# Moving the tiles of a one-core decoder step to other addresses in on-chip memory

## The chip, the cores and the metric

The kernel runs on one core of one Trainium2 chip. A core has engines that run side by side, each through its own list of instructions: TensorE (matrix products, PE in the profile, with its weight loads as PEld), VectorE (DVE), ScalarE (ACT), GpSimd (POOL) and SyncE (SP, which here issues most of the transfers). They share an on-chip memory of 128 partitions, called SBUF. A tile has one address, in bytes, which is the same in each partition. The metric is the device time of one execution, in microseconds (us).

## The reference

The reference is one inference step of a decoder layer, for 1024 prompt tokens and 8 x 8 sample tokens that share the weights, with a model width of 1024, all in 32-bit floats:

```python
u = rmsnorm(x); a, q, k, v, g_a, g_b = split(u @ w_in)
A = (multiscale_mean(a) - a) -> linear per group -> scale -> @ w_pa     # windows 2, 4, 8, 16
B = combine(dilated_attention(q_g, k_g, v_g) for g in 3 groups) @ w_pb  # (128,1) (512,4) (2048,16)
h = x + (sigmoid(g_a) * A + sigmoid(g_b) * B) @ w_o
y = h + relu(rmsnorm(h) @ w_up)**2 @ w_down
```

It also returns updated pooling rows and key and value windows for the prompt and for each sample.

## The kernel before, in words

Tokens are columns. The 1088 tokens stand in the free dimension, 1024 + 64, and a quarter of them is 272 columns. Nearly all the time goes into matrix products in TensorE's faster 32-bit format (`float32r` in the program). To keep the accuracy, each operand is split into a high and a low part, and each product is made of three passes, high x high, high x low and low x high (`PASSES`). A pass of one 128 x 128 block of weights over 272 tokens is one matmul instruction, which comes with one weight load. The operand that is loaded into the array is called stationary here, and the one that is streamed through it moving.

The stages, in order: the pooling projection (`pool_input`, line 326, tile `a`); queries, keys and values for the three attention groups with the attention around them (`gemm`, line 198, tiles `pq`, `pk`, `pv`, `pqk`); the two gates (`products`, line 1286, tile `pg`); the two branch projections (line 1592, `pab`); the output projection (`gemm`, `ph`); the up projection (`products`, `pz`); the down projection (line 2050, `pd`). Gates, up and down projection use a seven-product scheme in place of eight for a 2 x 2 division of the matrices. It forms sums of weight blocks and of activation blocks; the summed activations are called T1 to T4 in the code.

The tiles that the change touches, and where they stand:

- `places` (line 109) is the resident tile for weights, 48 KB of each partition, on the left side of the memory. Its three parts are filled in turn by ScalarE (high part) and VectorE (low part). Later the same bytes are reused at other offsets (`spots`) for weight blocks, for the sums T2 and T3, and in the down projection for the activations.
- `act_t` (line 83) are two tiles on the right side, high and low part of the activations. They are moving operand in `a`, `pg`, `ph`, `pz` and part of `pab`, and stationary operand in the query, key and value products of two of the groups.
- `ab0` (right side, below `act_t`) is moving operand in half of `pab`. `natt` (right side too) holds a copy of the activations that is the stationary operand for the first attention group.
- `xms`, `rtok`, `xeps` (lines 70 to 72) are seven small tiles of 9 columns with statistics per token, on the left side ahead of `places`.

A pool on the left side is stacked upwards and one on the right side downwards, in the order in which they are opened. A tile takes a multiple of 32 bytes. So the size of an early tile sets the address of all tiles opened after it on its side. Before the change, `places` stands at byte 21184, which is 192 over a multiple of 256, and 0 over a multiple of 64. The two activation tiles stand at 159712 and 194528, which is 224 over a multiple of 256 and 32 over a multiple of 64. A block of 128 in the contraction is 4352 bytes away from the next one in an activation tile, which is 17 x 256, and a quarter of the tokens is 1088 bytes, 17 x 64. So every address of a moving operand in the activation tiles is 32 over a multiple of 64 before the change. In `places` every operand starts at a multiple of 64.

The order of TensorE's work is the order of the code (the scheduler is told to leave that engine alone). The other engines' order is made by a scheduler.

Of the kernel before, what the change touches and what calls it, by code (L numbers as in the profile page):

```python
# [7 lines left out]
F32 = mybir.dt.float32  # L8
# [7 lines left out]
P = 128  # L16
# [20 lines left out]
def decoder_step(ctx, tc, i, o):  # L37
# [5 lines left out]
    def pool(name, bufs=1, **kw):  # L43
        return ctx.enter_context(tc.tile_pool(name=name, bufs=bufs, **kw))
# [9 lines left out]
    cp = pool("const")  # L54
# [12 lines left out]
    mhalf = cp.tile([P, 8], F32, name="mhalf")  # L67
    wqs = cp.tile([P, 6], F32, name="wqs")
    wqk = cp.tile([P, 6], F32, name="wqk")
    xms = cp.tile([P, 9], F32, name="xms")  # L70
    rtok = [cp.tile([P, 9], F32, name=f"rtok{g}") for g in range(3)]
    xeps = [cp.tile([P, 9], F32, name=f"xeps{g}") for g in range(3)]
    v_.memset(ones, 1.0)

    s_.activation(mhalf, ones[:, :8], AF.Copy)
# [5 lines left out]
    acts = ExitStack()  # L81
    actp = acts.enter_context(tc.tile_pool(name="act", bufs=1, side="right"))
    act_t = [actp.tile([P, KD, TOK], F32R, name=f"act{hl}") for hl in range(2)]
    act = [[t[:, k, :] for k in range(KD)] for t in act_t]
    act4 = [[t[:, k, :].rearrange("p (r l) -> p r l", r=4) for k in range(KD)] for t in act_t]

# [2105 lines left out]
```

## Time and profile before

| | |
|---|---|
| median of three runs | 1419.31 us (1417.27 to 1419.51) |
| span of the profiled execution | 1417.3 us; what lies around it can't be told from the runs, whose lowest is 1417.27 |
| TensorE busy | 1403.6 us, 99% of the span, 11101 matmuls |
| granted TensorE clock, mean | 0.998 |
| VectorE, ScalarE, GpSimd busy | 68%, 53%, 17% |
| share of the chain that ended last | PE 95%, DMA 2%, POOL 1%, ACT 1% |
| longest wait of TensorE for another engine | 3.2 us |

How to read it: the chain of waits is followed back from the last instruction, and gives each microsecond to the work that the end waited for. With 95% of it on TensorE, the time is the number of its matmuls times the spacing of their starts. The mean duration in a row (287 ns for 272 columns) is no cost, because matmuls are pipelined: the cost is the time from one start to the next. In the timeline each row gives a start, and the start of the next row less that of this one, divided by the count, is the spacing.

### The profile page before, as it was taken

The page shows a single profiled execution, that of the slowest core. Times are in us where ns is not written, and L with a number is a line of the kernel's source. Part 1 is how long each engine was busy: PE and PEld are TensorE (multiplying, and loading weights), DVE is VectorE, ACT ScalarE, POOL GpSimd, SP SyncE. Part 2 cuts the span into 40 slices and gives each one's busy share as a digit, 9 for nine tenths or more (in the row PEclk, how much of TensorE's full clock was granted, in tenths as well). Part 3 has the DMA queues.
Part 4 walks back from the last instruction along what each step waited for, and adds up shares of the span by engine and source line. Part 5 has one row for each costly group of instructions (what it writes and reads, how often), then busy time and mean ns, then how long its engine had stood idle before and what let it go on. Part 6 is the DMA issues. An engine that isn't in the chain of part 4 may idle for free.

```text
span 1417.3 us, 29517 instructions
## 1 busy us (share of the span) xinstructions
PE 1403.6 (99%) x11101; PEld 1355.2 (96%) x11101; DVE 967.3 (68%) x1766; ACT 758.0 (53%) x1962; POOL 235.6 (17%) x330
## 2 busy tenths in 40 slices
PE   9999999999999999999999999999999999999998
PEld 8988887887999999999999999999999999999998
DVE  7788666676676667876468677665665686664565
ACT  8557755777864323563336555454554545444443
POOL 0822275566500100000000000000000000000100
PEclk9999999999999999999999999999999999999999
DMA  6322789856477777965468668856758987777684
GB/s 213 116 92 104 206 219 223 206 129 143 109 251 225 247 231 236 323 226 174 132 199 288 224 219 270 263 199 209 246 191 273 326 270 259 227 244 226 204 257 167
DMA packets 184541, 303.58 MB, mean 214 GB/s; under 512 B 26567, under 2 KB 90509, under 8 KB 182350
## 3 DMA queue, kind: packets, MB, share of 16 engines
q1 hardware_dynamic: 181326, 258.04, 58.7%
q0 software_dynamic: 3072, 43.65, 9.6%
q8 instruction: 87, 1.43, 0.4%
q14 instruction: 56, 0.46, 0.1%
HBM read 231.55 MB, written 113.73 MB: 244 GB/s over the span
## 4 chain that ended last, share of the span: by engine, by line
PE 95%; DMA 2%; POOL 1%; ACT 1%; DVE 0%; issue 0%; SPq 0%; DVEq 0%; POOLq 0%; ACTq 0%
PE pz L1286 23%; PE pd L2050 23%; PE pg L1286 12%; PE ph L198 7%; PE pqk L198 6%; PE pab L1592 5%; PE pv L198 4%; PE a L326 4%; PE pq L198 2%; PE pk L198 1%; POOL pcv L849 1%; PE sg0b L682 1%; PE pog0b L715 1%; PE pl L505 1%; PE tpg0b L701 0%; POOL mr L644 0%
## 5 line engine op out<-in xcount | busy, mean ns | idle before, releaser
L2050 PE MATMUL pd<-places 128*128 128x272 f32 x2688 | 335.0, 287 | 0.5 <-DVE t L1914 0.5
L2050 PEld LDWEIGHTS pd<-places 128*128 128x128 f32 x2688 | 334.6, 188 | 0.7 <-DVE t L1914 0.7
L1293 ACT ACTIVATE places<-raw_d 128x544 fp32r<-128x544 f32 (+1 forms) x176 | 111.1, 646 | 164.3 <-DMA raw_d<-z_d 58.1
L1294 DVE TENSOR_TENSOR places<-raw_d,places 128x544 fp32r<-128x544 f32 (+1 forms) x176 | 122.9, 711 | 92.9 <-ACT places L1293 91.6
L2090 POOL DMA_DIRECT2D out_kv_sample_dram<-in_cache_kv_dram x96 | 47.2, 492 | 801.7 <-ACT places L1293 588.4
L1286 PE MATMUL pz<-act,places 128*128 128x272 f32 x1080 | 141.5, 289 | 0.0
L1286 PEld LDWEIGHTS pz<-act,places 128*128 128x128 f32 x1080 | 138.2, 188 | 0.0
L198 PE MATMUL ph<-act,places 128*128 128x272 f32 x768 | 97.0, 288 | 0.0
L198 PEld LDWEIGHTS ph<-act,places 128*128 128x128 f32 x768 | 96.5, 188 | 0.1
L1286 PE MATMUL pg<-act,places 128*128 128x272 f32 x576 | 76.6, 290 | 0.0
L1286 PEld LDWEIGHTS pg<-act,places 128*128 128x128 f32 x576 | 73.6, 188 | 0.6 <-issue 0.3
L1286 PE MATMUL pz<-places,apart 128*128 128x272 f32 x528 | 68.2, 287 | 0.0
L1286 PEld LDWEIGHTS pz<-places,apart 128*128 128x128 f32 x528 | 66.8, 188 | 0.0
L198 PE MATMUL pqk<-places,act 128*128 128x512 f32 x240 | 60.7, 403 | 0.0
L1286 PE MATMUL pz<-act,apart 128*128 128x272 f32 x456 | 59.9, 289 | 0.0
L1286 PEld LDWEIGHTS pz<-act,apart 128*128 128x128 f32 x456 | 58.3, 188 | 0.1
L198 PEld LDWEIGHTS pqk<-places,act 128*128 128x128 f32 x240 | 44.7, 192 | 9.8
L198 PE MATMUL pv<-places,act 128*128 128x256 f32 x384 | 50.4, 287 | 3.2 <-DVE places L115 3.2
L644 POOL TENSOR_TENSOR mr<-ms,mhalf 128x4 f32<-128x4 f32 (+2 forms) x39 | 53.0, 1359 | 3.1
L849 POOL TENSOR_TENSOR pck<-pck,qs 128x256 f32<-128x256 f32 x64 | 47.8, 779 | 31.6 <-DMA pck<-in_cache_kv_dram 17.1
L326 PE MATMUL a<-act,places 128*128 128x384 f32 (+1 forms) x288 | 50.8, 337 | 1.8 <-ACT places L114 1.0
L326 PEld LDWEIGHTS a<-act,places 128*128 128x128 f32 x288 | 49.2, 193 | 2.5 <-ACT places L114 1.3
(431 smaller groups left out, 2837.6 us busy)
## 6 DMA issues: line engine op xcount, KB each, us to landing
out_kv_sample_dram<-in_cache_kv_dram POOLq DMA_DIRECT2D x72, 480.0 KB, 5.0
raw_d<-z_d SPq DMA_DIRECT2D x112, 272.0 KB
z_d<-t SPq DMA_DIRECT2D x80, 272.0 KB
raw_d<-in_w_down_dram SPq DMA_DIRECT2D x80, 256.0 KB
raw_u<-in_w_up_dram SPq DMA_DIRECT2D x64, 256.0 KB
raw_qkv<-in_w_in_dram SPq DMA_DIRECT2D x36, 256.0 KB
pck<-in_cache_kv_dram SPq DMA_DIRECT2D x32, 256.0 KB
pcv<-in_cache_kv_dram SPq DMA_DIRECT2D x32, 256.0 KB
```

The source lines that it names most:

```text
L198: last_mm[0] = t_.matmul(out, lhs(a, k), rhs(b, k), start=(j == 0), stop=(j == len(terms) - 1))
L326: last_mm[0] = t_.matmul(pts[m][:, :n], wt[:, a, kk, m * P:(m + 1) * P], act4[b][kk][:, :, part4(c)], start=(p == 0 and kk == 0), stop=(p ...
L505: t_.matmul(pl[:, :npr], lin[:, g, :], dp_[:, c0:c0 + npr], start=True, stop=True)
L644: last_norm[0] = g_.tensor_tensor(r[:n, :H], ms[:n, :H], mhalf[:n, :H], op=ALU.pow)
L682: t_.matmul(sc[e][:, hp, j * P:(j + 1) * P], qT[rows, hp, :], kT[rows, 2 + hp, :], start=True, stop=True)
L849: ins = g_.tensor_tensor(out, *others, op=ALU.mult)
L1286: last_mm[0] = t_.matmul(x[c][:, :Q], A[:, a, k * P:(k + 1) * P], Bv(b, k, c), start=(first and n == 0), stop=(n == len(terms) - 1), skip_ ...
L1293: ins = s_.activation(view(t[:, 0]), src, AF.Copy)
L1294: v_.tensor_tensor(view(t[:, 1]), src, view(t[:, 0]).bitcast(F32), op=ALU.subtract)
L1592: last_mm[0] = t_.matmul(q[x][:, c, :Q], w.rearrange("p s n -> p (s n)")[:, at:at + P], rhs, start=(n == 0), stop=(n == len(terms) - 1))
L2050: last_mm[0] = t_.matmul(chain[t][:, c, :Q], A[:, a, t * P:(t + 1) * P], Z[:, b, c * Q:(c + 1) * Q], start=(fresh and f == 0 and n == 0), ...
L2090: ins = g_.dma_start(d, a)
```

## The change

Two edits, both to sizes. The seven small statistics tiles become seven slices of one tile of 64 columns: 256 bytes in place of 7 x 64 = 448 bytes. A tile of 56 columns (224 bytes) that nothing uses is opened below the activations on the right side.

```diff
-    xms = cp.tile([P, 9], F32, name="xms")
-    rtok = [cp.tile([P, 9], F32, name=f"rtok{g}") for g in range(3)]
-    xeps = [cp.tile([P, 9], F32, name=f"xeps{g}") for g in range(3)]
+    stats = cp.tile([P, 64], F32, name="stats")
+    xms, *per_token = (stats[:, 9 * n:9 * n + 9] for n in range(7))
+    rtok, xeps = per_token[:3], per_token[3:]
...
     act_t = [actp.tile([P, KD, TOK], F32R, name=f"act{hl}") for hl in range(2)]
+    actp.tile([P, 56], F32, name="act_end")
```

So every tile that is opened on the left side after `stats` moves down by 192 bytes, and every tile on the right side moves down by 224 bytes, for as long as the activations are held. `places` is then at 20992 and the activations at 159488 and 194304, all multiples of 256. `ab0` moves from 32 over a multiple of 64 to a multiple of 64, `natt` the other way, from a multiple of 64 to 32 over one. Each engine's list has the same instructions in the same order, with as many waits, before and after; only addresses differ. The names of lines below line 83 shift by one.

## The prediction

> **What bounds the kernel now.** I read the page first: busy time, granted clock and the chain that ended last.
>
> ```profile
> PE 1403.6 (99%) x11101; PEld 1355.2 (96%) x11101; DVE 967.3 (68%) x1766; ACT 758.0 (53%) x1962; POOL 235.6 (17%) x330
> PEclk9999999999999999999999999999999999999999
> PE 95%; DMA 2%; POOL 1%; ACT 1%; DVE 0%; issue 0%; SPq 0%; DVEq 0%; POOLq 0%; ACTq 0%
> ```
>
> TensorE is the bound in every stage, at full granted clock. The chain leaves 5% to other things. The list of TensorE's waits for other engines confirms it; these are its longest wait and the only one in the down projection:
>
> ```profile
> PE pv L198 <- DVE places L115: 3.2, 1, 3.2
> PE pd L2050 <- DVE t L1914: 0.5, 1, 0.5
> ```
>
> So no faster engine or transfer can give more than a few microseconds, and a change of addresses acts through one thing: the spacing of matmul starts. Two stretches of 100 us from the table by stage show how near it is to constant (columns: length, then busy time and count of PE, PEld, DVE, ACT, POOL, then clock, DMA share, GB/s):
>
> ```profile
> 500.00:600.00 100.00, 100.00 (x799) 100.00 (x799) 74.85 (x116) 40.93 (x66) 6.83 (x14) 1.00 0.80 263
> 1100.00:1200.00 100.00, 100.00 (x806) 100.00 (x805) 72.42 (x111) 47.94 (x79) 2.44 (x5) 1.00 0.86 283
> ```
>
> Nearly all of these matmuls stream 272 columns. In gates and branch projections (500 to 600 us) one takes 100/799 = 125.2 ns, in the down projection 100/806 = 124.1 ns. In the down projection both operands lie in `places`, at multiples of 64 bytes. In the gates more than half of the moving operands come from the activation tiles, which are 32 bytes off. That is the first sign of a price, about 1 ns, and the rest of the working is about what it is the price of.
>
> **The change part by part.** It removes no instruction, adds none and moves none; the lists of all engines read the same. What can change is what one instruction takes. I take the operands in groups.
>
> First, moving operands that come onto a multiple of 64. Their number is in the groups by shape:
>
> ```profile
> L1286 PE MATMUL pz<-act,places 128*128 128x272 f32 x1080 | 141.5, 289 | 0.0
> L198 PE MATMUL ph<-act,places 128*128 128x272 f32 x768 | 97.0, 288 | 0.0
> L1286 PE MATMUL pg<-act,places 128*128 128x272 f32 x576 | 76.6, 290 | 0.0
> L1286 PE MATMUL pz<-act,apart 128*128 128x272 f32 x456 | 59.9, 289 | 0.0
> L1592 PE MATMUL pab<-ab,places 128*128 128x272 f32 x384 | 50.5, 287 | 0.0
> L1592 PE MATMUL pab<-act,places 128*128 128x272 f32 x192 | 26.9, 289 | 0.0
> L1286 PE MATMUL pg<-act,gapart 128*128 128x272 f32 x192 | 25.5, 289 | 0.0
> L326 PE MATMUL a<-act,places 128*128 128x384 f32 x192 | 36.4, 351 | 1.8 <-ACT places L114 1.0 <-ACT act L304 0.9
> L326 PE MATMUL a<-act,places 128*128 128x320 f32 x96 | 14.8, 311 | 0.0
> L2050 PE MATMUL pd<-places 128*128 128x272 f32 x2688 | 335.0, 287 | 0.5 <-DVE t L1914 0.5
> ```
>
> With 272 columns that is 1080 + 768 + 576 + 456 + 192 + 192, and half of the 384 with `ab` (those of `ab0`), so 3456. The pooling projection `a` adds 192 + 96 = 288, which read four runs of 96 or 80 columns each.
>
> The price of one is read where both kinds follow each other, in the timeline of the gates (start, length, group, count):
>
> ```profile
> 501.22 3.19 PE L1286 MATMUL pg<-act,places 128*128 128x272 f32 x24
> 504.24 3.15 PE L1286 MATMUL pg<-gt,places 128*128 128x272 f32 x24
> 507.24 3.19 PE L1286 MATMUL pg<-act,gapart 128*128 128x272 f32 x24
> 510.26 3.15 PE L1286 MATMUL pg<-places,gapart 128*128 128x272 f32 x24
> 513.26 3.17 PE L1286 MATMUL pg<-places 128*128 128x272 f32 x24
> 516.26 3.19 PE L1286 MATMUL pg<-act,places 128*128 128x272 f32 x24
> 519.29 3.15 PE L1286 MATMUL pg<-gt,places 128*128 128x272 f32 x24
> 522.28 3.19 PE L1286 MATMUL pg<-act,gapart 128*128 128x272 f32 x24
> 525.31 3.15 PE L1286 MATMUL pg<-places,gapart 128*128 128x272 f32 x24
> 528.30 1.91 PE L1286 MATMUL pg<-places 128*128 128x272 f32 x14
> ```
>
> From start to start, the four blocks with `act` take 3.02, 3.02, 3.03 and 3.03, together 12.10 us for 96 matmuls or 126.0 ns each. The five others take 14.98 us for 120, or 124.8 ns. The difference is 1.2 ns. The chain of waits gives a second reading from long runs (start, length, group, count):
>
> ```profile
> 639.86 60.26 PE ph L198 x480
> 708.17 29.97 PE ph L198 x240
> 1082.57 330.31 PE pd L2050 x2652
> ```
>
> `ph` (moving operand in `act` throughout) is at 125.5 ns in the first run and 124.9 in the last, on average 90.23/720 = 125.3; `pd` is at 124.55. The difference is 0.8 ns, and 0.3 for the last run alone. I take 1.0 ns, between 1.2 and 0.8. The bounds are 0.3 and 126.0 - 124.1 = 1.9. That is 3456 x 1.0 = 3.5 us less, between 1.0 and 6.6.
>
> For the 288 of `a` no row shows the aligned case. They lose nothing at best, and at most four times 1.0 ns, one for each run: 0 to 1.2 us. I take the price of one run, 0.3 us.
>
> Second, stationary operands. The 672 + 240 query, key and value matmuls of two groups load their weights from `act`, which comes onto the grid; the 336 + 120 of the last group load from `natt`, which goes off it. Four blocks of 24 in the chain show both, the first two with `act`, the others with `natt`:
>
> ```profile
> 190.92 2.85 PE pv L198 x24
> 202.83 2.85 PE pv L198 x24
> 305.40 2.86 PE pv L198 x24
> 356.98 2.88 PE pv L198 x24
> ```
>
> Here the operand off the grid is the quicker one, 118.8 against 119.2 to 120.0 ns. So 912 lose and 456 gain 0.4 to 1.2 ns: 0.2 to 0.5 us more in sum. I take 0.3.
>
> Third, matmuls with both operands in tiles that stood at multiples of 64 already (`pd`, and the blocks with `gt`, `t` and `places`: 2688 + 1728 + 192). Both addresses move together, from 192 over a multiple of 256 to 0. In the timeline above the blocks without `act` agree within 0.01 us per 24, or 0.4 ns, though they use moving addresses at 0, 64, 128 and 192 over a multiple of 256. I take nothing, with 0.4 x 4608 = 1.8 us either way.
>
> The transfers, too, now land at other addresses, and VectorE and ScalarE write to them. That costs nothing on the path, because TensorE hides it. Only ahead of the first matmul nothing does, and there the chain has one transfer, of which a fraction could change:
>
> ```profile
> 2.13 4.68 DMA xs<-in_xT_dram
> ```
>
> Without the cover of TensorE, VectorE with 967 us of work would be next, far off.
>
> The sum is -3.5 - 0.3 + 0.3 = -3.5 us: 1417.3 becomes 1413.8 for the profiled execution. That one was at the lower edge of the runs (1417.27 to 1419.51), so against the median of 1419.3 I forecast **1415.8 us**. All bounds at once would give -6.6 - 1.2 + 0.2 - 1.8 = -9.4 to -1.0 + 0.5 + 1.8 = +1.3, which is 1409.9 to 1420.6; they will hardly come together, and I take 1411 to 1419 as the case's own range.
>
> **The rivals.** *The pattern counts, not the offset* (no change, 1419.3 us). In `act`, the blocks of one product are 4352 bytes apart, 17 x 256, so all start at the same place within 256 bytes; in the sums' tiles they are 2176 bytes apart and alternate between two places. The 1.2 ns may belong to that step, which the change keeps. For it speaks the last run of `ph`, which is off the grid and only 0.3 ns slower than `pd`. Against it speaks that every other block with `act` is slower than every block without.
>
> [...]
>
> *Both reads start together* (slower). Now activations and weights both stand at 0, 64, 128 or 192, with weights at 0. If TensorE's two reads get in each other's way when they start on the same grid, the blocks with `act` lose. The rows of `pv` show such a price: 120.0 against 118.8 ns, so 1.2 ns. On 3456 matmuls that is 4.1 us more, 1423.4 us. It decides from the point where blocks with `act` are above 126.0 ns. Against it: in the gates the blocks with both operands on the grid are the quicker ones.
>
> *The weights' multiple of 256 counts* (much faster). A weight load reads 512 bytes; from 192 over a multiple of 256 they lie in three pieces of 256, from 0 in two. If the spacing waits for the load, all products gain. The sample block of the key projection speaks against it, where loads of 128 and of 64 columns alternate (128x64 stands for the short one):
>
> ```profile
> 68.07 0.28 PE L623 MATMUL pk<-places,smp_t 128*64 128x256 f32 x1
> 68.18 0.28 PE L620 MATMUL pk<-places,smp_t 128*128 128x256 f32 x1
> 68.30 0.28 PE L623 MATMUL pk<-places,smp_t 128*64 128x256 f32 x1
> 69.35 0.28 PE L620 MATMUL pk<-places,smp_t 128*128 128x256 f32 x1
> ```
>
> The next start comes 0.12 us after either, so half a load saves nothing between neighbours. But this block is at (69.35 - 68.07)/11 = 116.4 ns, and full loads over as many columns are at 118.8, so lighter loads may save 2.4 ns on average. At that price 8064 matmuls of 272 columns would give 19 us, 1400 us.
>
> **How the numbers follow.** Forecast 0.52, no change 0.27, slower by collision 0.13, weights' multiple 0.08. A difference under 0.2%, here 2.8 us, can't be told from none. Of the forecast's range the larger part, some three quarters, lies beyond that: 0.40 of the 0.52. With 0.08 of the last rival and 0.02 from the edge of the second, *faster* gets 0.50. *Same* gets 0.12 + 0.25 + 0.01 = 0.38, *slower* 0.12. The range goes from 1408.5 us, which takes in the forecast's bounds and more than half of the last rival's gain, to 1420.5 us, which takes in no change with the spread of the runs and leaves out most of the collision.
>
> **What would show it.** In the timeline of the gates the blocks with `act` should come down from 3.02 or 3.03 to 3.00 us, with the others as they are; the first run of `ph` should take 59.8 rather than 60.3 us for its 480; the stretch from 1100 to 1200 us should keep its 806 matmuls; the waits of TensorE should stay as they are. Blocks with `act` that stay at 3.02 mean the pattern, at 3.05 the collision. More than 810 matmuls from 1100 to 1200 would mean the weights' multiple, and the forecast would be wrong by most of its size.

## The result and the profile after

The changed kernel took 1415.44 us (median of 18 runs, 1411.76 to 1420.20) and the kernel before, timed along with it, 1417.88 (18 runs, 1415.81 to 1421.69). The ratio is 0.9979, with a 95% interval of 0.9970 to 0.9989: 2.4 us or 0.2% faster on the medians, between 1.6 and 4.3 by the interval. The same kernel with one more comment, timed again later (the last experiment), came out at 0.9994 (0.9980 to 1.0009). The two ratios weighted by the squares of their intervals give 0.9984 +- 0.0008, or 2.3 us with 1.2 to 3.5.

The profiled execution has a span of 1411.4 us, where before's has 1417.3. That is more than the change gives, and the first thing to find out is where the 5.9 us lie. The page of the changed kernel:

```profile
PE 1400.8 (99%) x11101; PEld 1351.8 (96%) x11101; DVE 964.9 (68%) x1766; ACT 758.4 (54%) x1962; POOL 234.4 (17%) x330
PE 90%; DMA 4%; DVE 3%; ACT 1%; issue 1%; POOL 1%; SPq 1%; DVEq 0%; POOLq 0%; ACTq 0%
```

TensorE has the same 11101 matmuls and is the bound as before, though the chain now gives it 90% where it had 95: it passes through more of the waits early on. Two rows of its list of waits for other engines, in the changed kernel:

```profile
PE pog1b L716 <- ACT pTg1b L705: 1.9, 2, 1.6
PE pv L199 <- DVE places L116: 1.1, 1, 1.1
```

The wait of `pv` for `places` is 2.1 us shorter than in the profile of before, and the wait of `pd` for `t` (0.5 us) is not there. The long runs in the chain that ended last (start, length, group, count), first of before, the two groups that the prediction didn't show, then of the changed kernel:

```profile
420.13 147.51 PE pg L1286 x1176
749.24 322.33 PE pz L1286 x2568
```

```profile
415.40 147.41 PE pg L1287 x1176
635.29 60.45 PE ph L199 x480
703.79 30.00 PE ph L199 x240
744.92 327.49 PE pz L1287 x2616
1072.40 334.54 PE pd L2051 x2688
```

The long run of the gates starts at 415.40 in place of 420.13. So 4.7 of the 5.9 us lie ahead of it, in the part with the attention, where TensorE waits for others. From there on the gates take 147.41 us for 147.51, the output projection 60.45 and 30.00 for 60.26 and 29.97, the up projection 125.19 ns per matmul for 125.52, the down projection 334.54/2688 = 124.46 ns. These are differences of tenths of a microsecond, but for the up projection's 0.33 ns x 2616 = 0.9 us.

The 4.7 us can't be put down to the change. The same two rows in the second profile of the changed kernel (the last experiment; chain, then waits):

```profile
420.70 147.41 PE pg L1287 x1176
```

```profile
PE pv L199 <- DVE places L116: 3.2, 1, 3.2
```

Here the gates start at 420.70, later than in the kernel before, with the wait of `pv` back at 3.2 us, and its span is 1416.6 us. The gates' own 147.41 us are the same to the last digit. Over the fourteen profiles of this study that start lies anywhere from 415.40 to 420.70 us, and two executions of the changed kernel alone stand at these two ends. So a single profile says nothing on the part ahead of the gates to less than some 5 us, while the times of the stages behind it repeat to some tenths of a microsecond. Both profiles with the addresses of before start the gates late, at 420.13 and 420.57 us; the twelve with other addresses start them at 418.1 us on average. That the change shortens this part by a microsecond or two is therefore neither shown nor excluded.

Now the rows that the prediction rests on. The timeline of the gates, changed kernel:

```profile
496.47 3.16 PE L1287 MATMUL pg<-act,places 128*128 128x272 f32 x24
499.47 3.16 PE L1287 MATMUL pg<-gt,places 128*128 128x272 f32 x24
502.46 3.16 PE L1287 MATMUL pg<-act,gapart 128*128 128x272 f32 x24
505.46 3.16 PE L1287 MATMUL pg<-places,gapart 128*128 128x272 f32 x24
```

From start to start the blocks with `act` take 3.00 us, nearly as those without (2.99 and 3.00): they came down from 3.02 or 3.03 as forecast. But other blocks with `act` went the other way. The timeline at the start of the gates and of the up projection, before and then changed:

```profile
419.97 27.28 PE L1286 MATMUL pg<-act,places 128*128 128x272 f32 x216
447.09 3.15 PE L1286 MATMUL pg<-act,gapart 128*128 128x272 f32 x24
...
752.08 9.22 PE L1286 MATMUL pz<-act,places 128*128 128x272 f32 x72
761.14 6.21 PE L1286 MATMUL pz<-act,apart 128*128 128x272 f32 x48
```

```profile
419.78 22.86 PE L1287 MATMUL pg<-act,places 128*128 128x272 f32 x180
442.49 3.17 PE L1287 MATMUL pg<-act,gapart 128*128 128x272 f32 x24
...
747.76 9.24 PE L1287 MATMUL pz<-act,places 128*128 128x272 f32 x72
756.84 6.22 PE L1287 MATMUL pz<-act,apart 128*128 128x272 f32 x48
```

In the gates (447.09 - 419.97)/216 = 125.6 ns became (442.49 - 419.78)/180 = 126.2, in the up projection 125.8 became 126.1. What sets these blocks apart is the quarter of the tokens that they read: the early ones read the first two quarters of the activation tiles, the ones from 497 us on the last two.

Since the order of TensorE's instructions is the same in both kernels, each matmul can be paired with itself. This table is worked out from the single records of the trace: mean time from one start to the next in ns, by stage and quarter of `act`, without the few places where TensorE waited. (A row of the timeline merges the two quarters of a block.) The distance is the address of the moving operand less that of the stationary one, modulo 256: 32, 96, 160 and 224 for the four quarters before, 0, 64, 128 and 192 now.

```
                          count   before   changed   in sum, us
pg, act, quarter 0          192   125.88   126.01      +0.02
pg, act, quarter 1          192   125.39   126.32      +0.18
pg, act, quarter 2          192   125.95   126.02      +0.01
pg, act, quarter 3          192   125.98   123.68      -0.44
pz, act, quarter 0          384   125.58   125.58       0.00
pz, act, quarter 1          384   126.14   125.96      -0.07
pz, act, quarter 2          384   125.60   126.07      +0.18
pz, act, quarter 3          384   126.08   123.62      -0.94
ph, act, quarter 0          192   125.81   125.82       0.00
ph, act, quarter 1          192   125.63   126.49      +0.17
ph, act, quarter 2          192   123.65   126.56      +0.56
ph, act, quarter 3          192   126.06   123.51      -0.49
pab, act                    192   126.39   125.03      -0.26
pab, ab0                    192   125.01   125.52      +0.10
pd                         2688   124.45   124.45       0.00
pv pq pk, natt, 256 columns        119.53   117.03     -0.78
pqk, natt, 512 columns             229.89   232.93     +0.32
pv pq pk, act, 256 columns         119.2    119.0      -0.16
pqk, act, 512 columns              233.3    232.6      -0.15
all groups                                              -1.7
```

The 3456 matmuls of the prediction's first term give 0.98 us less, 0.28 ns each. The quarter at distance 192 gains 2.3 to 2.6 ns, and most others stay or lose. The rest of the 1.7 us is with the products whose stationary operand is `natt`. These rows of the timeline show that (before, then changed):

```profile
352.14 3.01 PE L198 MATMUL pqk<-places,natt 128*128 128x512 f32 x12
...
356.74 3.12 PE L198 MATMUL pv<-places,natt 128*128 128x256 f32 x24
```

```profile
348.32 3.06 PE L199 MATMUL pqk<-places,natt 128*128 128x512 f32 x12
...
352.97 3.06 PE L199 MATMUL pv<-places,natt 128*128 128x256 f32 x24
```

A block of 24 with 256 columns went from 3.12 to 3.06 us, 2.5 ns each; a block of 12 with 512 columns from 3.01 to 3.06, 4 ns each the other way.

### The profile page after: what moved, and what is told of

Its sections match the earlier page's. It is cut to its first block, busy times and chain, and to the rows that moved or that the text cites. A ratio compares the mean times of both kernels' runs of the same rounds, so it can differ in the third digit from the quotient of the medians.

```text
span 1411.4 us, 29517 instructions
## 1 busy us (share of the span) xinstructions
PE 1400.8 (99%) x11101; PEld 1351.8 (96%) x11101; DVE 964.9 (68%) x1766; ACT 758.4 (54%) x1962; POOL 234.4 (17%) x330
## 4 chain that ended last, share of the span: by engine, by line
PE 90%; DMA 4%; DVE 3%; ACT 1%; issue 1%; POOL 1%; SPq 1%; DVEq 0%; POOLq 0%; ACTq 0%
PE pz L1287 24%; PE pd L2051 24%; PE pg L1287 12%; PE ph L199 7%; PE pqk L199 6%; PE pv L199 4%; PE a L327 3%; PE pq L199 1%; PE pab L1593 1%; PE pk L199 1%; DMA gg<-g_d 1%; DMA raw_qkv<-in_w_in_dram 1%; PE sg0b L683 1%; DVE gg L1598 1%; PE pog0b L716 1%
## 5 line engine op out<-in xcount | busy, mean ns | idle before, releaser
L1593 PE MATMUL pab<-ab,places 128*128 128x272 f32 x384 | 50.8, 288 | 0.1
```

The source lines that it names most:

```text
L1593: last_mm[0] = t_.matmul(q[x][:, c, :Q], w.rearrange("p s n -> p (s n)")[:, at:at + P], rhs, start=(n == 0), stop=(n == len(terms) - 1))
```

## The experiments

The first question is whether offsets over a multiple of 64 or 256 count at all, or only how the two operands stand to each other.

**The kernel before again.** A comment more, nothing else.

> The kernel before, once more, with no edit but a comment. Both theories, that of the grid (a moving operand that starts off a multiple of 64 bytes costs about 1 ns) and that of the distance (only the start of the moving operand less that of the stationary one, modulo 256 bytes, sets the spacing), expect the stages after 420 us as before: gates blocks with act at 3.02 or 3.03 us, 806 matmuls from 1100 to 1200 us. What differs from before ahead of 420 us shows how far two executions of one kernel differ there: under 2 us if the 4.7 us that the changed kernel gained there belong to the change, 3 us or more if they come from one execution to the next.

1419.03 us against 1417.63 for the kernel before, ratio 1.0004 (0.9986 to 1.0023). The spacings agree with the first profile of before to 0.01 ns in nearly every group of the table (pg quarters: 125.87, 125.39, 125.95, 125.98), and their sum to 0.1 us. So differences of a few tenths of a ns between these groups can be read from one profile, though times can't be told apart to better than some 2 us.

```profile
420.57 147.46 PE pg L1287 x1176
```

The gates start 0.4 us later than in the first profile of before. By the expectation, a difference under 2 us would speak for the change as the cause of the 4.7 us. The second profile of the changed kernel speaks against it: the same layout started its gates at 415.40 us and at 420.70.

**Activations alone.** In the kernel before, only the activation tiles move, by 32 bytes, to 192 over a multiple of 256, where the weights stand:

```diff
     act_t = [actp.tile([P, KD, TOK], F32R, name=f"act{hl}") for hl in range(2)]
+    actp.tile([P, 8], F32, name="act_end")
```

> The kernel before with the activations alone moved by 32 bytes, so that they stand at 192 over a multiple of 256, as the weights do; the statistics tiles are not packed. Grid and distance both expect the stages of the changed kernel, since the activations are on a multiple of 64 and at distance 0 from the weights: gates blocks with act at 3.00 (T1, 22) and ph at 60.4 us for its first 480. A theory by which the weights' multiple of 256 has a part expects some of the gain missing. Time about 1415.5 us.

1416.4 us, ratio 0.9983 (0.9967 to 1.0). The sum of spacings is 1.86 us below before, the changed kernel's 1.66. By quarter the gates are at 125.65, 126.28, 126.02 and 123.68 ns, within 0.4 of the changed kernel, though the weights stand at 192 over a multiple of 256. So the multiple of 256 under the weights has no effect that shows here.

**Weights alone.** The changed kernel without the unused tile beside the activations:

```diff
-    actp.tile([P, 56], F32, name="act_end")
```

> The changed kernel without the tile below the activations: weights at a multiple of 256, activations at 224 over one as before. Grid: nothing gained, gates blocks with act at 3.02 or 3.03 as before, time about 1418 us. Distance: the distances of the two halves of the activations, 32 and 96 for the first and 160 and 224 for the second before, become 224 and 32, and 96 and 160, so the blocks of the gates with act (second half) fall from 3.03 to about 3.015 us, and those of the up projection with the first half rise by as much; sum unchanged within 1 us.

1416.84 us, ratio 0.9984 (0.9968 to 1.0), spacings 1.96 us below before in sum. Here the activations keep their 32 bytes off the grid of 64, and the gain is the same. The distances are 224, 32, 96 and 160, and the quick quarter is again the last, at 160: 124.05 ns in the gates, 124.03 in the up projection, 123.73 in the output projection. In the kernel before the distance of 160 (third quarter) was quick only in the output projection (123.65) and not in the gates (125.95): the distance isn't the whole of it.

**Everything 32 bytes off.** The changed kernel's distances, with all of it moved off the grid:

```diff
+    cp.tile([P, 8], F32, name="shift")
     stats = cp.tile([P, 64], F32, name="stats")
...
-    actp.tile([P, 56], F32, name="act_end")
+    actp.tile([P, 48], F32, name="act_end")
```

> The changed kernel with everything moved up by 32 bytes: weights and activations both start 32 over a multiple of 64, at the same distances from each other as in the changed kernel. Grid: all 8064 matmuls of 272 columns pay 1 ns, the down projection falls from 806 to 800 matmuls in 100 us, the gates blocks with act are at 3.02 to 3.03, and the time is about 1420 to 1423 us. Distance: every stage as in the changed kernel, 806 and 3.00, time about 1415.5 us.

By spacings this decides: pg 126.07, 126.34, 126.02 and 123.68, pz 125.63, 125.98, 126.05 and 123.63, ph 125.83, 126.49, 126.54 and 123.50, all within 0.1 ns of the changed kernel, with no operand of these products on a multiple of 64. So the grid of 64 bytes has no price in these products, and what counts is how the two operands stand to each other. In sum the spacings are 1.3 us below before. The time can't show it: 1417.73 us, ratio 0.9996 (0.9977 to 1.0014), which holds the changed kernel's ratio and 1 both.

**Activations 64 bytes further.** The changed kernel with a smaller unused tile beside them, so that the distances are 64, 128, 192 and 0 by quarter:

```diff
-    actp.tile([P, 56], F32, name="act_end")
+    actp.tile([P, 40], F32, name="act_end")
```

> The changed kernel with the activations 64 bytes higher: the four quarters at distance 64, 128, 192 and 0 instead of 0, 64, 128 and 192, all on multiples of 64. Grid: no change. Distance: each quarter takes over the spacing that another had at that distance, in the up projection 126.0, 126.1, 123.6 and 125.6 ns instead of 125.6, 126.0, 126.1 and 123.6, so the first run of 480 of ph stays and its last 240 get shorter or longer by less than 0.4 us; sum unchanged within 0.5 us, about 1415.4 us.

The quick quarter moved to the third: gates 126.47, 126.31, 123.45, 125.76; up projection 126.36, 126.27, 123.48, 125.77; output projection 126.58, 126.46, 123.49, 125.59. The spacings of the changed kernel, turned by one quarter, come back within 0.4 ns. The time is 1416.34 us, ratio 0.9987 (0.9975 to 0.9999). So for the blocks with `act` of these three stages, a distance of 192 gives 123.5 ns and 0, 64 or 128 give 125.6 to 126.6, and both layouts have one good quarter of four. The sum did not stay within 0.5 us, as the expectation had it: paired with before as in the table, the spacings are 0.3 us less here, where the changed kernel's are 1.7 us less. The up projection and the products with `natt` gain some 0.4 us less each; the rest is with the branch projections and the pooling projection, of which the second differs between executions of one kernel too.

**The down projection by distance.** Its moving operands lie in `places` at all four distances in turn, at 124.45 ns. Two kernels give it two distances only, in the one 0 and 128, in the other 64 and 192, by other places for the activations of that stage. The diff is the first one's; the second has 1040 in place of 1024 in `tz`, which is 64 bytes more:

```diff
-        at = (8704, 0, 2112, 4224, 6336)[spot[1] % 5]
-        return put(hi_lo(at, 512), w, marks_f), put(hi_lo(at + 1024, H), z, marks_f)
+        at = (8960, 0, 2240, 4480, 6720)[spot[1] % 5]
+        tw = put(hi_lo(at, 512), w, marks_f)
+        tz = spots[:, at + 1024:at + 1024 + 2 * 608].rearrange("p (s n) -> p s n", s=2)[:, :, :576].rearrange("p s (c n) -> p s c n", c=2)[:, :, :, :Q]
+        ins = s_.activation(tz[:, 0], two(z), AF.Copy)
+        v_.tensor_tensor(tz[:, 1], two(z), tz[:, 0].bitcast(F32), op=ALU.subtract)
...
-                    last_mm[0] = t_.matmul(chain[t][:, c, :Q], A[:, a, t * P:(t + 1) * P], Z[:, b, c * Q:(c + 1) * Q],
+                    last_mm[0] = t_.matmul(chain[t][:, c, :Q], A[:, a, t * P:(t + 1) * P], Z[:, b, c],
```

> The changed kernel with the activations of the down projection laid out so that moving operands stand at distance 0 and 128 from their weights in turn (0, 128, 0 for the first quarter, 128, 0, 128 for the second), where the changed kernel has 0, 128, 0 and 64, 192, 64. All stay on multiples of 64. Grid: no change, 806 matmuls from 1100 to 1200 us, 1415.4 us. Distance: the spacing that the sums' blocks have at 0 and 128 in turn, 123.3 ns instead of 124.45, so 811 matmuls in that stretch, 3.0 us less for 2688 of them, about 1412.4 us.

> As the run before, but with those activations 64 bytes further on, so at distance 64 and 192 in turn, still all on multiples of 64. Grid: no change, 1415.4 us. Distance: the spacing that the sums' blocks reach at 64 and 192 in turn, 126.5 ns, so 790 matmuls from 1100 to 1200 us, 5.5 us more, about 1421 us.

The first took 1416.62 us, ratio 0.9988 (0.9973 to 1.0003), the second 1420.24, 1.0017 (1.0004 to 1.0031). The chain and one window of the first, then the chain of the second:

```profile
1074.40 336.02 PE pd L2056 x2688
```

```profile
1100.00:1200.00 100.00, 100.00 (x803) 100.00 (x802) 72.28 (x111) 47.63 (x78) 2.92 (x6) 1.00 0.85 279
```

```profile
1074.72 337.50 PE pd L2056 x2688
```

The stage became slower in both, 336.02 us (125.00 ns) and 337.50 (125.56), where 123.3 ns had been expected of the first, from blocks with summed activations that alternate between these two distances. Not all of those blocks were that quick: the first halves of the gates' blocks with both operands in `places` do the same at 125.0 ns. So the distance doesn't set the spacing by itself, and the theory of the distance, as it stood, fell here.

**The weights moved for half the tokens.** To the first of these two kernels, 128 bytes are added to the place of the weights that meet the first half of `act` (in the gates to 12 of 16 blocks), so that its second quarter comes to the distance of 192 too:

```diff
-            w = put(hi_lo(1024 * (n % 3), 512), raw_first.pop(n), marks_g)
+            w = put(hi_lo(1088 * (n % 3) + 32, 512), raw_first.pop(n), marks_g)
...
-    up_spots = [spots[:, 8704 + 1024 * n:9728 + 1024 * n].rearrange("p (s n) -> p s n", s=2) for n in range(3)] + apart
+    up_spots = [spots[:, 8704 + 1088 * n:9792 + 1088 * n] for n in range(3)]
+    up_spots += [up.tile([P, 1088], F32R, name=f"apart{n}") for n in range(2)]
...
-            return put_up(first_quarter(f, a)) if early and m == 0 else put_up(quarter(f, m, a), True)
+            return put_up(first_quarter(f, a), by=32) if early and m == 0 else put_up(quarter(f, m, a), True, 32 * (1 - m))
```

> The run at 0 and 128 (e4), and besides the weights that meet the first half of the activations moved by 128 bytes (in the up projection all, in the gates 12 of 16), so that this half stands at distance 128 and 192 instead of 0 and 64. Grid: no change, 1415.4 us. Distance: spacing of that half from 125.8 to 124.85 ns for 768 + 288 matmuls, 1.0 us more than e4 gains, together 4.0 us less than the changed kernel, about 1411.4 us.

1415.83 us, ratio 0.9981 (0.9967 to 0.9994), where 1411.4 us had been expected. For blocks with `act` the distance holds again: second quarter 124.23 ns in the gates and 123.73 in the up projection (126.32 and 125.96 before this edit), first quarter 126.27 and 126.43 at 128, in sum 0.9 us less. The gates hold a comparison within one run: the 12 blocks whose weights moved give 123.6 ns for the second quarter, the 4 whose weights stayed 126.3, where all 16 had 126.3 in the changed kernel. The surprise is in the down projection, whose addresses are those of the kernel above. The chain shows it in two pieces:

```profile
1075.42 143.14 PE pd L2056 x1145
1221.00 188.24 PE pd L2056 x1524
```

```profile
1100.00:1200.00 100.00, 100.00 (x802) 100.00 (x801) 72.02 (x110) 46.85 (x78) 2.92 (x6) 1.00 0.84 276
1200.00:1300.00 100.00, 99.92 (x808) 99.70 (x807) 59.94 (x90) 44.22 (x74) 6.81 (x14) 1.00 0.76 235
1300.00:1400.00 100.00, 100.00 (x813) 100.00 (x812) 62.74 (x92) 48.19 (x80) 7.29 (x15) 1.00 0.69 220
```

The first 1145 matmuls go at 143.14/1145 = 125.0 ns, the later ones at 123.5 with the end of the last one in it (123.33 between starts). The clock is 1.00 throughout. At the border TensorE paused once, for ScalarE's copy of a finished tile:

```profile
1221.00 3.13 PEld L2056 LDWEIGHTS pd<-places 128*128 128x128 f32 x25 [0.30 <-ACT park_b L1982]
```

One start came 369 ns behind the one before, the next 230. Ahead of it the starts repeat 125, 128, 123, 124 ns, behind it 128, 119, 123, 123, until the end. So one pattern of addresses has two rhythms, and the move from one to the other came with a pause. By the single records, the spacings of this profile sum to 3.2 us less than before's, more than those of the changed kernel, but the time doesn't show it.

**Matmuls cut in two.** To test that, 21 of the down projection's 2688 matmuls are cut into two by columns, three in each of the seven products, at 136, 68, 204, 32, 240, 16 and 256 in turn, in the layout with distances 0 and 128 and in the changed kernel:

```diff
+                    cut = []
+                    if f in (2, 6, 10) and (t, c, n) == (0, 0, 1):
+                        cut = [(136, 68, 204, 32, 240, 16, 256)[cuts[0] % 7]]
+                        cuts[0] += 1
+                    for lo, hi in zip([0] + cut, cut + [Q]):
+                        last_mm[0] = t_.matmul(chain[t][:, c, lo:hi], A[:, a, t * P:(t + 1) * P], Z[:, b, c, lo:hi],
```

> e4's layout of the down projection (distances 0 and 128 in turn), in which 21 of the 2688 matmuls are cut into two by columns, three in each of the seven passes, at 136, 68, 204, 32, 240, 16 and 256 of the 272 columns in turn. Each cut breaks the rhythm of starts for a moment. Theory 'rhythm': matmuls in a row fall into a rhythm that lasts until something breaks it, and one pattern of addresses has more than one such rhythm. Then stretches between cuts stand at different spacings, 125.0 ns (e4) or 123.3 ns (the last part of the run of both layouts, behind a wait of 0.4 us), each constant from one cut to the next; with half of them at 123.3 the down projection takes 2688 x 0.85 ns = 2.3 us less than e4's 336.0 us, and 21 x some 0.1 us = 2 us more for the cuts, so nothing in sum. Theory 'something else at that time' (transfers, another engine): the cuts change nothing, spacing stays at 125.0 in all stretches or changes away from cuts; 338 us.

> The changed kernel with the same 21 cuts. Its down projection (distances 0 and 128 for one tile, 64 and 192 for the next) kept 124.45 ns through every wait so far, in all runs. Theory 'rhythm': this pattern has one rhythm that all starts fall back into: 124.45 ns in all stretches, up to some ten matmuls behind a cut, 334.5 us + 21 x 0.1 = 336.6 us for the down projection, time 1417.5 us. If stretches differ here too, the spacing of the down projection, equal before and after the change, was equal by chance of its entry.

From the single records, spacing in each stretch that follows a cut, in its later part (ns; three stretches for each cut; the first stretch of the first kernel, ahead of all cuts, was at 123.3, where the same layout without cuts had been at 125.0 from its start):

```
cut at column          136    68    204   32    240   16    256
distances 0 and 128   125.0  123.3  125.0 125.0 123.4 123.3 123.3
changed kernel        124.5  124.5  124.5 124.5 124.5 124.5 124.5
```

All three stretches behind a cut at the same column agree within 0.1 ns. Two windows of the first kernel, of 35 us each, the one behind cuts at 204 and 32, the other behind cuts at 16 and 256:

```profile
1103.50:1138.50 35.00, 35.00 (x283) 35.00 (x282) 26.02 (x41) 16.20 (x28) 0.00 (x0) 1.00 0.92 302
1151.50:1186.50 35.00, 35.00 (x286) 35.00 (x285) 26.36 (x41) 16.80 (x29) 1.95 (x4) 1.00 0.84 273
```

The second has three more in the same time. The same windows of the changed kernel with its cuts:

```profile
1103.50:1138.50 35.00, 35.00 (x284) 35.00 (x283) 26.53 (x41) 16.45 (x27) 0.00 (x0) 1.00 0.92 299
1151.50:1186.50 35.00, 35.00 (x284) 35.00 (x283) 25.62 (x40) 17.48 (x30) 1.95 (x4) 1.00 0.81 261
```

No difference there. So the rhythm theory holds on both counts: the layout with two distances has two spacings that last, and the normal layout of the down projection falls back to one, 124.45 ns, within some thirty matmuls. (The stretch ahead of all cuts repeats 120, 126, 121, 126 ns, so the spacing of 123.3 has more than one pattern.) That is why that stage was equal before and after the change, and in all kernels that left its layout alone. The times are 1415.13 us, ratio 0.9985 (0.9972 to 0.9998), and 1416.86 us, 0.9996 (0.9984 to 1.0008).

**One cut for the quicker rhythm.** The kernel with the weights moved for half the tokens, with one cut at column 16 near the start of the down projection:

```diff
+                    cut = [16] if p == 2 and f == 2 and (t, c, n) == (0, 0, 1) else []
```

> e7 (the down projection with distances 0 and 128 in turn, half of the weights that meet the activation tiles 128 bytes further) with one matmul near the start of the down projection cut at column 16, the cut that led to 123.3 ns three times out of three. Theory 'rhythm': 123.3 ns through the whole down projection unless a wait changes it, 331.5 us against 336.0 without the cut and 334.5 in the changed kernel, 811 matmuls from 1100 to 1200 us; the time goes 3 us below the changed kernel's, and the better activation blocks of e7 (c1 at 124.2 and 123.7 ns for 126.3 and 126.0) take 1 us more: 1411.4 us where the changed kernel takes 1415.4. Theory 'place in time': spacing goes back to 125.0 by itself; 1415.8 us as e7.

1416.55 us, ratio 0.9990 (0.9971 to 1.0008), and the whole stage at 125.0 ns:

```profile
1076.18 336.13 PE pd L2058 x2689
```

The expectation left out what stood ahead of each cut in the run above. There the cut at 16 had always come behind the cut at 240, so the quicker rhythm was already there; here it came upon 125.0 ns, and 125.0 stayed. In all four cases the cut at 16 kept what it found. The cuts that were seen to lead from 125.0 to 123.3 are those at 68 and 240, three times each. One of them in this place wasn't tried, so no version of this study is shown to beat the time of the changed kernel.

**The changed kernel again.**

> The changed kernel again, with a comment more. Theory 'spacing and chance': spacings as in the first profile to 0.1 ns per group (gates with act 126.0, 126.3, 126.0 and 123.7 ns by quarter), but the part ahead of the gates, whose waits differ from one execution to the next, comes out between 375.6 and 380 us rather than at 375.6 again; time 1415.5 to 1416.5 us, 1.5 to 2.5 below before. Theory 'the change shortens the part ahead of the gates': 375.6 us again within 0.5, and the wait of pv for places again near 1.3 us.

1417.11 us against 1418.08, ratio 0.9994 (0.9980 to 1.0009). The gates repeat at 126.02, 126.32, 126.01 and 123.68 ns, and the part ahead of them didn't repeat, as the rows in the first section show. One group differs within the same kernel: the pooling products with 384 columns, at 176.2 ns in the first profile and 178.0 in this one. So this stage had one spacing in one execution and another in the next, with nothing changed. This group takes most of the difference in the sum: the spacings of the second profile are 1.2 us below before's, those of the first 1.7.

## Why the prediction was right in its number and wrong in its reason

The forecast of 1415.8 us is 0.4 us from the median, and the 3.5 us that it was made of is inside the first interval (1.6 to 4.3) and at the edge of the two timings together (1.2 to 3.5). That closeness is luck. The forecast started from 1419.3 us, a median of three runs, where eighteen give 1417.88: 1.4 us too high. It took off 3.5 us where the medians differ by 2.4: 1.1 us too much. The two errors nearly cancel. And the spacings gain 1.2 to 1.7 us, mostly elsewhere than forecast.

**The bound** was read rightly: TensorE's spacing at full clock (granted 0.998 on average in the profile of before, 0.999 in that of the changed kernel), nothing else. The transfers and the other engines changed nothing that repeats. The sum of spacings, 1.7 us in one profile and 1.2 in the other, lies at the lower end of the interval of both timings (1.2 to 3.5 us); what is left up to their 2.3 us is inside the noise, and could also lie ahead of the gates.

**The first term** (3456 matmuls come onto a multiple of 64 and gain 1.0 ns each, 3.5 us) is the step that failed, in what it said is the price and on whom it falls. It measured 0.28 ns each, 0.98 us. The price was read in four blocks of the gates between 501 and 529 us, and these four did lose it: 126.0 ns became 125.0. But they read the last two quarters of `act` only, and of these two the one at distance 192 alone gained. The row at 420 us in the timeline of before, which the prediction doesn't use, has 216 matmuls with `act` at 125.6 ns, another kind already by its number. The prediction's own last run of `ph` at 124.9 ns, off the grid and quick, was the same hint: its third quarter was at 123.65 ns, at a distance of 160. Not the grid of 64 but the distance of the two operands modulo 256 sorts the blocks with `act`, as the kernel with everything 32 bytes off and those with the activations or the weights moved alone show.

**The second term** (`a`, 0.3 us less) measured under 0.1 us of change in the first profile and some 0.35 us more in the second, so no gain is shown. The second has 2 ns more for each matmul of 384 columns in the same kernel.

**The third term** (stationary operands, 0.3 us more) had the wrong sign. Products with `act` as the stationary operand, which came onto the grid, gained 0.1 to 0.3 us, by profile, where a loss was forecast; those with `natt`, which went off it, gained 0.78 with 256 columns and lost 0.32 with 512. Together that is 0.6 to 0.8 us less. The 0.4 to 1.2 ns that this term used were differences between blocks in one layout, and again said nothing on the grid.

**The fourth term** (both operands on the grid already: no change) held: 0.00 us in the down projection and under 0.05 us in the other blocks.

**The rivals.** *The pattern counts* said that the blocks with `act` would stay at 3.02 us; those that it meant came down to 3.00. It was right against the forecast that the grid is no cause. But the address counts all the same: the quarters of `act`, with blocks 4352 bytes apart in each, differ by up to 3 ns (`ph` of the changed kernel, 126.56 and 123.51). *Both reads start together* had the sign right for the blocks with the second quarter in `pg` and `ph` (125.4 to 126.3 and 125.6 to 126.5), but not for a common grid: at distance 0 nothing changed. *The weights' multiple of 256* is refuted by the down projection, whose weights came onto such a multiple and which kept its 806 matmuls, and by the kernel that moved the activations alone and has the gain.

**What should have shown it.** The gates' blocks at 3.00 came; the first run of `ph` at 59.8 did not, it went from 60.26 to 60.45; 806 matmuls from 1100 to 1200 us stayed. The waits of TensorE were to stay as they are, and did not in the one profile, by 2.1 us in one place, but that wait was 3.2 us again in the next execution.

What makes the starts settle in a rhythm, and why 192 is a good distance for the blocks with `act`, and 160 in some places, is open. The single records of before and of the changed kernel show that a weight load (188 ns in its row) starts 122 ns ahead of its matmul and 3 ns after the start of the matmul before it (medians of 8058 matmuls with 272 columns in each), so the rows of a load and of the matmul before it overlap in all but one of these 8058; whether either holds up the other was not tried.

## What to carry to other kernels

A price of 1 ns per matmul that is read from a few neighbouring blocks is a price of these blocks: sort all matmuls of the kind by every property of their addresses before it is multiplied by thousands. Two profiles of one kernel should be laid side by side before a difference in one of them is explained: here spacing repeats to 0.1 ns in almost every group, while the part with waits differs by 5 us between executions. Moving tiles by some bytes was worth a tenth or two of a percent in this kernel, which is bound by matmul spacing, and which way it goes couldn't be told from alignment alone.

## What the runs showed of the hardware

- Spacing of matmuls with 272 columns in this 32-bit format, each with its own weight load, lay between 123.3 and 126.6 ns in the groups of the table above, in all runs, at full clock (granted 0.997 to 1.000 on average by profile). For the blocks with `act` of the gates, the up and the output projection its mean by quarter follows the distance between the moving and the stationary operand modulo 256 bytes (192: 123.5 to 123.7 ns; 0, 64 and 128: 125.6 to 126.6), and not the alignment of either to 64 or 256 bytes. At 160 both kinds were seen: 123.65 ns and 125.95 in two stages of one kernel.
- Starts fell into a rhythm that repeats, for instance 125, 128, 123, 124 ns, over the first 1145 matmuls of the down projection in one run. In the changed kernel's down projection, 99.8% of the spacings are within 1 ns of the one 36 matmuls before. One set of addresses had two spacings that last (125.0 and 123.3 ns with distances 0 and 128 in turn). A matmul cut in two at column 68 or 240 moved TensorE from the slower to the quicker one, three times each, and a cut at 136 or 204 back; the one such move without a cut came with a start that was 369 ns behind the one before.
- With four distances in turn (the down projection as it is) there was one rhythm in every profile, 124.45 ns, also after 21 cuts.
- With 256 columns the spacing went from 119.5 to 117.0 ns and with 512 from 229.9 to 232.9 by the same change of addresses, with the stationary operand in `natt`.
